# Hybrid decoder step: the first weight half between the first two row sets, two squares later

## The chip, the cores and the metric

The kernel runs on one core of a Trainium2 chip. The metric is the device time of one launch in microseconds (us). PE is TensorE, DVE is VectorE, ACT is ScalarE, POOL is GpSimd, SP is SyncE, whose queue issues most of the transfers here.

## What is computed

One layer of a decoder for a prompt of 512 rows and a sample group of 8 rows, each of width 1024. The part that matters here is the beginning: each row is normalised and multiplied with the input projection.

```python
def rms_norm(x, w):
    xf = x.astype(jnp.float32)
    y = xf * lax.rsqrt(jnp.mean(xf * xf, axis=-1, keepdims=True) + RMS_EPS)
    return (y * w.astype(jnp.float32)).astype(x.dtype)
...
    h = rms_norm(x, norm_w)
    z = jnp.einsum('bsd,de->bse', h, w_in)
    u, g_ssm, q, g_nsa, kv, gl = jnp.split(z, IN_SPLITS, axis=-1)
```

After that come a state-space scan over `u`, three branches of attention (compressed, selected and window) for prompt and sample, and one output projection with the residual.

## The kernel before, in words

The prompt's 512 rows are four row sets `xts[0..3]` of 128 rows by 1024 columns; in the listings below they are `x_66` to `x_69`. PE transposes a row set in eight 128x128 pieces (`x_transposes`), so that the 1024 columns lie on the partitions as eight slices k = 0 to 7. Two row sets together fill four PSUM banks, two with the tag `c` and two with the tag `t`; bank `t_143` can only be used once ACT has copied the transposed norm weights `nwT` out of the bank of the same tag.

Every product is computed in three matmuls of rounded parts (`mm3`, lines 121 to 123: high by high, high by low, low by high). So each operand is split in two: ACT writes the rounded high part, DVE subtracts it and writes the low part. For rows this is `x_split` (ACT `hTh`, DVE `hTl`), which multiplies with `nwT` on the way; for weights it is `w_split` (ACT `whi`, DVE `wlo`). The factor 1/rms of each row is not applied to the rows but to the results: `square` sums the squares of a row set (on ACT or DVE), `rstd_of` turns the sum into the factor with a scale on DVE and a power on POOL, and `row_table` transposes the factors so that they can be multiplied in. The sample rows `xs_in` are scaled first (`sample_scale`), transposed and split too (`sample_split`).

The first weights, 1024 by 256 columns, come in two halves (`prep_load`): k = 0 to 3 and k = 4 to 7. `u_mm` with `chan_mm(first=True)` uses them in two passes: the first over the first two row sets (`x_66`, `x_67`; 48 matmuls), the second over the other two and the sample columns (264 columns).

What sets the order: the program is written in one order, and a scheduler that is given that order and its own costs places the instructions on each engine. At the start `in_turn` binds it: each step may only be issued after the one before it on the engines of both. `issue_after` does the same for single instructions. `warm` puts matmuls without use on PE: nine at the beginning, three after the transposes of the first row set and two after those of the second. [...]

```python
square(S, ssd[0], xts[0], 128)
square(V, ssd[1], xts[1], 128)
tail = [square(S, sss, xs_in, 8)]
```

These three lines (279 to 281) put the squares of the first two row sets and of the sample rows ahead of everything in `in_turn`.

Of the kernel before, what the change touches and what calls it, by code (L numbers as in the profile page):

```python
# [26 lines left out]
C_ID, C_GRP, C_CAUS, C_CMASK, C_ROPE = 0, 128, 192, 320, 448  # L27
# [9 lines left out]
def hymba_step_kernel(  # L37
# [8 lines left out]
    nc = tc.nc  # L46
# [19 lines left out]
    V, S = PsumFirst(nc.vector), PsumFirst(nc.scalar)  # L66
# [7 lines left out]
    last = {}  # L74

    def nm(p):
        cnt[0] += 1
        return f"{p}{cnt[0]}"

    def ht(name, cols=1024, dt=F32, parts=128):  # L80
        return big.tile([parts, cols], dt, tag="H", name=nm(name), bufs=NH)

    def pt_(name, cols=1024, dt=F32, parts=128):
        return big.tile([parts, cols], dt, tag="P", name=nm(name), bufs=NP)

    def ld(name, cols=1024, dt=F32, parts=128):
        return big.tile([parts, cols], dt, tag="ld", name=nm(name), bufs=NLD)

    def wh(name, cols=1024):
        return big.tile([128, cols], F32R, tag="wh", name=nm(name), bufs=NWH)  # L90

    def st(shape, name, dt=F32, bufs=1, tag=None):
        n = nm(name)
        return sm.tile(shape, dt, tag=tag or n, name=n, bufs=bufs)
# [7 lines left out]
    def k1(name, cols=128, parts=128, dt=F32):  # L102
        return sm.tile([parts, cols], dt, tag="k1", name=nm(name), bufs=NS)
# [6 lines left out]
    def pb(use):  # L110
        tag = ROUTE[use]
        return psum.tile([128, 512], F32, tag=tag, name=nm(tag), bufs=BANKS[tag])
# [32 lines left out]
    xts = [ht("x") for _ in range(4)]  # L145
    cst = st([128, NC_CST], "cst")
    nwr = k1("nwr", 128, 8)
    xs_in = pt_("xs", parts=8)
# [6 lines left out]
    load_x = lambda i: nc.sync.dma_start(xts[i], x_prompt[0, 128 * i:128 * i + 128, :])  # L155
    nc.scalar.dma_start(nwr, norm_w.rearrange("o (a n) -> (o a) n", a=8))
    load_x(0)
    nc.sync.dma_start(cst[:, 0:128], cst_d[:, 0:128])
    load_x(1)
    nc.sync.dma_start(xs_in, x_sample[:, 0, :])  # L160
    ident = cst[:, C_ID:C_ID + 128]

    mhalf = st([128, 16], "mhalf")
    V.memset(mhalf, -0.5)
# [1 line left out]
    def rstd_of(out, ssq, n, parts, cols):  # L166
        V.tensor_scalar(out, ssq, 1.0 / n, EPS, op0=ALU.mult, op1=ALU.add)
        return G.tensor_tensor(out, out, mhalf[:parts, :cols], op=ALU.pow)  # L168
# [28 lines left out]
    p = pb("tr")  # L197
# [6 lines left out]
    def square(eng, ss, xtile, parts):  # L204
        if eng is V:
            return V.scalar_tensor_tensor(xsq[1][:parts], xtile, 1.0, xtile, op0=ALU.mult, op1=ALU.mult, accum_out=ss)
        return S.activation(xsq[0][:parts], xtile, AF.Square, accum_out=ss)
# [9 lines left out]
    def x_split(j, banks, k):  # L217
        sl = slice(256 * j, 256 * j + 256)
        p = banks[k % 4][:, 256 * (k // 4):256 * (k // 4) + 256]
        h = S.mul(hh(k)[:, sl], p, nwT[:, k:k + 1])  # L220
        return h, V.scalar_tensor_tensor(hl(k)[:, sl], p, nwT[:, k:k + 1], hh(k)[:, sl].bitcast(F32), op0=ALU.mult, op1=ALU.subtract)

    rsd = st([128, 4], "rsd")
    rsT = st([128, 512], "rsT", tag="rsT")

    w_in2 = w_in[0]

    def prep(c0, n=256, cols=None, use=None):

        return list(prep_steps(c0, n, cols, use))[-1]  # L230

    def prep_load(c0, n=256, cols=None):
        v = lambda t: t.rearrange("p (k n) -> p k n", n=n)
        parts = []
        for k0, nk in (((0, 4), (4, 4)) if n == 256 else ((0, 3), (3, 3), (6, 2))):
            raw = ld("w", nk * n)
            src = w_in2[128 * k0:128 * (k0 + nk)].rearrange("(k p) n -> p k n", p=128)
            for o, c, m in cols or ((0, c0, n),):
                last["load"] = nc.sync.dma_start(v(raw)[:, :, o:o + m], src[:, :, c:c + m])
            parts.append((raw, k0, nk))  # L240
        return parts

    def prep_steps(c0, n=256, cols=None, use=None):
        v = lambda t: t.rearrange("p (k n) -> p k n", n=n)
        tiles = []
        parts = prep_load(c0, n, cols)
        yield
        for raw, k0, nk in parts:
            if use:
                use(v(raw), k0, nk)  # L250
            hi, lo = wh("whi", nk * n), wh("wlo", nk * n)
            split(hi, lo, raw)
            tiles += [(v(hi)[:, k], v(lo)[:, k]) for k in range(nk)]
        yield tiles


    w0 = [(raw, wh("whi"), wh("wlo")) for raw, _, _ in prep_load(0)]
    load_x(2)
    load_x(3)

    def w_split(k, n):
        raw, hi, lo = w0[k // 4]
        sl = slice(256 * (k % 4), 256 * (k % 4) + 256 * n)
        h = S.copy(hi[:, sl], raw[:, sl])
        return h, V.tensor_tensor(lo[:, sl], raw[:, sl], hi[:, sl].bitcast(F32), op=ALU.subtract)
# [4 lines left out]
    ssd, sss = [st([128, 1], "ss", bufs=4, tag="ss") for _ in range(4)], st([8, 1], "ss8")  # L270
    rs = st([8, 1], "rs")
    b0 = x_banks()
# [4 lines left out]
    with tc.issue_after(last["xt"].ins):  # L277
        warm(NFILL - 1)
    square(S, ssd[0], xts[0], 128)
    square(V, ssd[1], xts[1], 128)  # L280
    tail = [square(S, sss, xs_in, 8)]
    for i in range(2):
        rstd_of(rsd[:, i:i + 1], ssd[i], 1024, 128, 1)
    rstd_of(rs, sss, 1024, 8, 1)

    def in_turn(*steps):

        for f in steps:
            with ExitStack() as s_:
                for i_ in tail:  # L290
                    s_.enter_context(tc.issue_after(i_.ins))
                new = f()
            tail[:] = list(new) if len(new) > 1 else tail if not new else [i_ for i_ in tail if i_.ins.engine != new[0].ins.engine] + list(new)
# [4 lines left out]
    def row_table(i):  # L298
        if i == 0:
            pr[0] = pb("ph")  # L300
        rb = k1("rb")
        c_ = V.tensor_copy(rb, rsd[:, i:i + 1].to_broadcast([128, 128]))
        T.transpose(pr[0][:, 128 * i:128 * i + 128], rb, ident)
        if i % 2:
            S.copy(rsT[:, 128 * i - 128:128 * i + 128], pr[0][:, 128 * i - 128:128 * i + 128])
        return (c_,)
# [12 lines left out]
    def sample_split():  # L319
        for kp in range(4):  # L320
# [5 lines left out]

    x = lambda j, b, k: lambda: x_split(j, b, k)
    w = lambda k, n: lambda: w_split(k, n)
    in_turn(x(0, b0, 0), x(0, b0, 1), w(0, 1), x(0, b0, 2), w(1, 1), x(0, b0, 3), w(2, 2), sample_scale, x(0, b0, 4), x(0, b0, 5),
            w(4, 2), lambda: row_table(0), lambda: row_table(1), x(0, b0, 6), x(0, b0, 7), w(6, 2), sample_split,  # L330
            lambda: (square(S, ssd[2], xts[2], 128),), lambda: (square(S, ssd[3], xts[3], 128),))
    b1 = x_banks()
    for i in range(2):
# [167 lines left out]
    p = pb("ac")  # L501
# [123 lines left out]
    for src, ct_ in ((c_re, CTr), (c_im, CTi)):  # L625
        cn = k2("cn", 256).rearrange("p (q n) -> p q n", n=64)
        nc.sync.dma_start(cn, src[0].rearrange("(q g) c n -> (g c) q n", q=4))
        p = pb("ac")
# [18 lines left out]
    for a, src in enumerate((state_re, state_im)):  # L647
        n0 = k1("n0")
        nc.sync.dma_start(n0, src[0].rearrange("b (a c) n -> (b a) (c n)", c=2))
        p = pb("ac")  # L650
# [312 lines left out]
    p = pb("tr")  # L963
# [794 lines left out]
```

## Time and profile before

| | |
|---|---|
| median of 3 runs | 468.19 us (467.05 to 469.04) |
| the profiled execution | 468.64 us, span 466.9 us |
| PE busy | 452.1 us, 97% of the span |
| DVE busy | 348.8 us, 75% |
| ACT busy | 241.3 us, 52% |
| POOL busy | 95.4 us, 20% |
| mean granted TensorE clock | 0.985 of full |

The span runs from the first to the last instruction of the profiled execution; its own time has a little around it. An engine's busy share is a mean over stages with different limits. Times in the rows below are counted from the start of the span.

### The profile page before, as it was taken

What the parts mean: (1) busy time and instruction counts of PE and PEld (TensorE: products, weight loads), DVE (VectorE), ACT (ScalarE), POOL (GpSimd) and SP (SyncE); (2) the same over time, 40 slices, a digit from 0 to 9 for tenths busy, and PEclk for the clock granted to TensorE, in tenths of its full rate; (3) what the DMA queues carried; (4) which work ended last, traced back from release to release, by engine and by line L of the source; (5) the groups of instructions that cost most, each with busy time, mean ns of one, the idle gap of its engine ahead of it and who ended that gap; (6) DMA issues with size and microseconds to landing.
All of it is one profiled execution on the core that took longest, in us unless ns stands there. A gap on an engine that the chain in (4) does not pass through costs nothing.

```text
span 466.9 us, 10954 instructions
## 1 busy us (share of the span) xinstructions
PE 452.1 (97%) x4258; PEld 385.9 (83%) x4258; DVE 348.8 (75%) x942; ACT 241.3 (52%) x587; POOL 95.4 (20%) x104
## 2 busy tenths in 40 slices
PE   8999999999999998799999999999899999999996
PEld 4989999899999998698686776867568799799885
DVE  6978999998998998385676858687756687683332
ACT  5913764756324328475676668566856555342100
POOL 3100000056442000462342214321433010000000
PEclk9999999999999997789999999999999999999999
DMA  8776533614627433466143362429343784311211
GB/s 290 247 225 167 84 73 108 187 40 82 143 57 214 129 82 73 148 209 187 46 140 114 121 215 79 148 90 350 104 141 130 220 209 152 101 58 58 69 46 48
DMA packets 75635, 62.84 MB, mean 135 GB/s; under 512 B 29262, under 2 KB 69056, under 8 KB 75456
## 3 DMA queue, kind: packets, MB, share of 16 engines
q1 hardware_dynamic: 66208, 36.74, 28.2%
q0 software_dynamic: 4816, 17.03, 11.5%
q10 hardware_dynamic: 4560, 8.39, 5.7%
q8 instruction: 33, 0.54, 0.5%
q14 instruction: 18, 0.15, 0.1%
HBM read 55.63 MB, written 10.70 MB: 142 GB/s over the span
## 4 chain that ended last, share of the span: by engine, by line
PE 73%; DVE 13%; DMA 7%; POOL 3%; issue 2%; ACT 1%; SPq 0%; DVEq 0%; POOLq 0%; ACTq 0%
PE a L121 11%; PE a L122 11%; PE a L123 10%; PE ph L1372 8%; DMA kvg<-in_cache_kv_dram,idx 4%; PE a L1262 4%; PE t L1253 4%; PE a L1220 3%; PE t L1348 3%; PE c L1545 3%; POOL rsq L168 2%; DVE ga L62 2%; PE t L1338 2%; PE ph L473 1%; DMA x<-in_x_prompt_dram 1%
## 5 line engine op out<-in xcount | busy, mean ns | idle before, releaser
L121 PE MATMUL a<-hTh,whi 128*128 128x256 f32 (+1 forms) x192 | 54.8, 287 | 0.6 <-DVE sg L61 0.6
L122 PE MATMUL a<-hTh,wlo 128*128 128x256 f32 (+1 forms) x192 | 54.8, 287 | 0.0
L123 PE MATMUL a<-hTl,whi 128*128 128x256 f32 (+1 forms) x192 | 53.4, 284 | 0.0
L1329 POOL DMA_INDIRECT kvg<-in_cache_kv_dram,idx x32 | 32.8, 1026 | 82.2 <-PE c L1123 40.1
L168 POOL TENSOR_TENSOR rsq<-rsq,mhalf 128x6 f32<-128x6 f32 (+3 forms) x10 | 28.7, 2872 | 101.8 <-DVE rsq L62 101.8
L122 PE MATMUL a<-whi,hTl 128*128 128x256 f32 (+1 forms) x160 | 45.8, 287 | 0.0
L123 PE MATMUL a<-wlo,hTh 128*128 128x256 f32 (+1 forms) x160 | 45.3, 284 | 0.0
L121 PE MATMUL a<-whi,hTh 128*128 128x256 f32 (+1 forms) x160 | 45.2, 287 | 0.0
L1372 PE MATMUL ph<-XT,W1h 128*128 128x256 f32 x256 | 44.5, 298 | 0.0
L61 ACT ACTIVATE P<-a,mx 128x128 f32<-128x128 f32 (+3 forms) x64 | 33.6, 533 | 13.3 <-DVE mx L61 11.5
L61 DVE TENSOR_REDUCE mx<-a 128x1 f32<-128x384 f32 (+3 forms) x48 | 27.9, 596 | 13.8 <-PE a L1221 13.6
L121 PEld LDWEIGHTS a<-hTh,whi 128*128 128x128 f32 x192 | 36.2, 188 | 1.1 <-DVE sg L61 0.8
L122 PEld LDWEIGHTS a<-hTh,wlo 128*128 128x128 f32 x192 | 36.2, 188 | 0.9 <-issue 0.4
L122 PE MATMUL a<-woh,mixl 128*128 128x256 f32 x128 | 36.1, 283 | 0.0
L121 PE MATMUL a<-woh,mixh 128*128 128x256 f32 x128 | 36.1, 284 | 0.0
L123 PE MATMUL a<-wol,mixh 128*128 128x256 f32 x128 | 36.0, 283 | 0.0
L123 PEld LDWEIGHTS a<-hTl,whi 128*128 128x128 f32 x192 | 35.7, 189 | 0.1
L1372 PEld LDWEIGHTS ph<-XT,W1h 128*128 128x128 f32 x256 | 34.9, 192 | 0.3 <-ACT XT L61 0.2
L62 ACT CAST whi<-w 128x1024 fp32r<-128x1024 f32 (+4 forms) x26 | 23.9, 927 | 15.8 <-PE a L122 10.5
L61 ACT COPY pT<-t 128x512 f32<-128x512 f32 x40 | 23.1, 588 | 15.8 <-PE t L1253 12.6
L122 PEld LDWEIGHTS a<-whi,hTl 128*128 128x128 f32 x160 | 30.1, 188 | 1.2 <-issue 0.9
L121 PEld LDWEIGHTS a<-whi,hTh 128*128 128x128 f32 x160 | 29.9, 189 | 0.9 <-PE ph L473 0.4
(410 smaller groups left out, 1235.5 us busy)
## 6 DMA issues: line engine op xcount, KB each, us to landing
w<-in_w_in_dram SPq DMA_DIRECT2D x16, 512.0 KB
out_dram<-in_cache_win_dram ACTq DMA_DIRECT2D x8, 511.0 KB
x<-in_x_prompt_dram SPq DMA_DIRECT2D x4, 512.0 KB
TT<-scr_k SPq DMA_DIRECT2D x4, 512.0 KB
w<-in_w_in_dram SPq DMA_DIRECT2D x16, 128.0 KB
W1r<-in_cmp_w_dram SPq DMA_DIRECT2D x4, 512.0 KB
wk<-in_cache_win_dram SPq DMA_DIRECT2D x8, 256.0 KB
wv<-in_cache_win_dram SPq DMA_DIRECT2D x8, 256.0 KB
```

The costliest lines, as they stand in the source:

```text
L61: return f(*args, **kw)
L62: return f(*args, **kw)
L121: T.matmul(out, ah, bh, start=start, stop=False, skip_group_check=True)
L122: T.matmul(out, al, bh, start=False, stop=False, skip_group_check=True)
L123: T.matmul(out, ah, bl, start=False, stop=stop, skip_group_check=True)
L168: return G.tensor_tensor(out, out, mhalf[:parts, :cols], op=ALU.pow)
L1220: T.matmul(bank, QTv(g, r)[:, qsl], KTv(g, a)[:, brs, :n], start=(a == 0), stop=False, skip_group_check=True)
L1253: T.transpose(p[:, 128 * r:128 * r + 128], P[r][:, br, 128 * kt:128 * kt + 128], ident)
L1262: mm = T.matmul(po[64 * br:64 * br + 64, :], kvt[kt - 1][:, c0:c0 + 64], behind[kt - 1][br][0], start=(kt == 1), stop=(kt == i + 1), tile_ ...
L1329: G.indirect_dma_start(out=gt_, out_offset=None, in_=ckv, in_offset=bass.IndirectOffsetOnAxis(ap=idx[:, 2 * pr_ + b2, jq:jq + 1], axis=0))
L1348: T.transpose(p[:, 256 * g + 128 * b2:256 * g + 128 * b2 + 128], gts[jq][b2][:, o:o + 128], ident)
L1372: T.matmul(ph3[:, kd], (W1l if part == 1 else W1h)[kd][a][:, wsl], (xl if part == 2 else xh)[:, e, a:a + 256], start=(jq == 0 and kd == 0 ...
```

## The change

The transfer of the first half of the weights is issued ahead of the second row set, and the second half behind it; `prep_load` gets a hook between its two halves for that. The sample rows are fetched after both. In `in_turn` the splits of k = 0 to 3 of the weights now stand ahead of all splits of rows, and the squares of the second row set (DVE) and of the sample rows (ACT), with the two factors that come out of them, have become a step of `in_turn` behind the split of k = 4 and 5 of the weights. The rest of the diff is code that only stands at another line.

```diff
-    load_x(1)
-    nc.sync.dma_start(xs_in, x_sample[:, 0, :])
...
-    def prep_load(c0, n=256, cols=None):
+    def prep_load(c0, n=256, cols=None, between=None):
...
             parts.append((raw, k0, nk))
+            if between:
+                between()
+                between = None
         return parts
+    first_w = prep_load(0, between=lambda: load_x(1))
+    nc.sync.dma_start(xs_in, x_sample[:, 0, :])
...
-    w0 = [(raw, wh("whi"), wh("wlo")) for raw, _, _ in prep_load(0)]
+    w0 = [(raw, wh("whi"), wh("wlo")) for raw, _, _ in first_w]
...
     square(S, ssd[0], xts[0], 128)
-    square(V, ssd[1], xts[1], 128)
-    tail = [square(S, sss, xs_in, 8)]
-    for i in range(2):
-        rstd_of(rsd[:, i:i + 1], ssd[i], 1024, 128, 1)
-    rstd_of(rs, sss, 1024, 8, 1)
+    tail = []
+    rstd_of(rsd[:, 0:1], ssd[0], 1024, 128, 1)
+    def rows_squared():
+        i_ = square(V, ssd[1], xts[1], 128), square(S, sss, xs_in, 8)
+        rstd_of(rsd[:, 1:2], ssd[1], 1024, 128, 1)
+        rstd_of(rs, sss, 1024, 8, 1)
+        return i_
...
-    in_turn(x(0, b0, 0), x(0, b0, 1), w(0, 1), x(0, b0, 2), w(1, 1), x(0, b0, 3), w(2, 2), sample_scale, x(0, b0, 4), x(0, b0, 5),
-            w(4, 2), lambda: row_table(0), lambda: row_table(1), x(0, b0, 6), x(0, b0, 7), w(6, 2), sample_split,
+    in_turn(w(0, 1), w(1, 1), w(2, 2), x(0, b0, 0), x(0, b0, 1), x(0, b0, 2), x(0, b0, 3), x(0, b0, 4), w(4, 2), rows_squared,
+            x(0, b0, 5), sample_scale, lambda: row_table(0), lambda: row_table(1), x(0, b0, 6), x(0, b0, 7), w(6, 2), sample_split,
```

How the order moves on ACT, from its first square on (`w_124` and `w_82` are the first half of the weights, `w_126` and `w_85` the second, `c_140` to `t_143` the banks of transposed rows). Before:

```order
L62 ACTIVATE xsq_120,ss_134<-x_66 128x1024
L62 ACTIVATE xsq_120,ss_138<-xs_72 8x1024
L61 COPY nwT_118<-t_116 128x8
L61 ACTIVATE hTh_108<-c_140,nwT_118 128x256
L61 ACTIVATE hTh_108<-t_141,nwT_118 128x256
L62 CAST whi_128<-w_124 128x256
L61 ACTIVATE hTh_109<-c_142,nwT_118 128x256
```

With the change:

```order
L62 ACTIVATE xsq_124,ss_134<-x_66 128x1024
L62 CAST whi_128<-w_82 128x256 x2
L62 CAST whi_128<-w_82 128x512
L61 COPY nwT_122<-t_120 128x8
L61 ACTIVATE hTh_112<-c_140,nwT_122 128x256
L61 ACTIVATE hTh_112<-t_141,nwT_122 128x256
L61 ACTIVATE hTh_113<-c_142,nwT_122 128x256
L61 ACTIVATE hTh_113<-t_143,nwT_122 128x256
L61 ACTIVATE hTh_114<-c_140,nwT_122 128x256
L62 CAST whi_130<-w_85 128x512
L62 ACTIVATE xsq_124,ss_138<-xs_72 8x1024
```

The three casts of the first half have moved ahead of the copy `nwT`, and the square of the sample rows has moved behind five row splits and a cast.

On PE, from the last transpose of `x_66` that needs no `nwT` (`wz` are the fill matmuls). Before:

```order
L213 MATMUL c_142<-cst_70,x_66 128x128
L213 MATMUL c_140<-cst_70,x_67 128x128
...
L213 MATMUL c_142<-cst_70,x_67 128x128
L213 MATMUL t_143<-cst_70,x_66 128x128 x2
L177 LDWEIGHTS wz_86
L177 MATMUL ph_88<-wz_86 128x512
...
L213 MATMUL t_143<-cst_70,x_67 128x128 x2
```

With the change:

```order
L230 MATMUL c_142<-cst_70,x_66 128x128
L230 MATMUL t_143<-cst_70,x_66 128x128 x2
L194 LDWEIGHTS wz_90
L194 MATMUL ph_92<-wz_90 128x512
...
L230 MATMUL c_140<-cst_70,x_67 128x128
L230 MATMUL t_141<-cst_70,x_67 128x128
L230 MATMUL c_142<-cst_70,x_67 128x128
L230 MATMUL t_143<-cst_70,x_67 128x128
```

Six transposes of `x_67` have moved from ahead of `t_143` and the three fill matmuls to behind them.

On SP, the first transfers (`cst_70` is the table of constants, `xs_72` the sample rows). Before:

```order
L155 DMA x_66<-in_x_prompt_dram 128x1024
L158 DMA cst_70<-in_constants_dram 128x128
L155 DMA x_67<-in_x_prompt_dram 128x1024
L160 DMA xs_72<-in_x_sample_dram 8x1024
L239 DMA w_124<-in_w_in_dram 128x4x256
L239 DMA w_126<-in_w_in_dram 128x4x256
```

With the change:

```order
L155 DMA x_66<-in_x_prompt_dram 128x1024
L158 DMA cst_70<-in_constants_dram 128x128
L170 DMA w_82<-in_w_in_dram 128x4x256
L155 DMA x_67<-in_x_prompt_dram 128x1024
L170 DMA w_85<-in_w_in_dram 128x4x256
L178 DMA xs_72<-in_x_sample_dram 8x1024
```

One half of the weights has moved ahead of `x_67`, the other ahead of the sample rows.

## Rows read from the trace of the kernel before

**Rows 1.** The page, part 4: the chain that ended last, shares by engine.

```profile
PE 73%; DVE 13%; DMA 7%; POOL 3%; issue 2%; ACT 1%; SPq 0%; DVEq 0%; POOLq 0%; ACTq 0%
```

**Rows 2.** The chain in order of time: start us, us, what.

```profile
1.64 5.81 DMA x<-in_x_prompt_dram
...
10.95 0.12 PE a L122
...
13.74 0.59 PE ph L314 x8
...
14.91 0.44 PE t L213 x4
...
98.83 1.15 DVE pt L62 x2
```

**Rows 3.** Timeline of PE, 6 to 19 us: start us, us, what, [idle before].

```profile
6.49 0.42 PE L213 MATMUL c<-cst,x 128*128 128x128 f32 x1
7.49 0.33 PE L213 MATMUL c<-cst,x 128*128 128x128 f32 x1 [0.58 <-DMA x<-in_x_prompt_dram]
...
8.58 0.44 PE L213 MATMUL t<-cst,x 128*128 128x128 f32 x2 [0.21 <-ACT nwT L61]
8.86 0.81 PE L177 MATMUL ph<-wz 128*128 128x512 bf16 x3
9.50 0.38 PE L213 MATMUL t<-cst,x 128*128 128x128 f32 x2
...
9.96 0.47 PE L121 MATMUL a<-hTh,whi 128*128 128x256 f32 x1
...
19.00 0.29 PE L121 MATMUL a<-hTh,whi 128*128 128x264 f32 x1
```

**Rows 4.** Timeline of ACT, 7 to 14 us.

```profile
7.33 1.06 ACT L62 ACTIVATE xsq<-xs 8x1024 f32<-8x1024 f32 x1 [1.71 <-DMA xs<-in_x_sample_dram]
...
8.39 0.14 ACT L61 COPY nwT<-t 128x8 f32<-128x8 f32 x1
8.56 0.47 ACT L61 ACTIVATE hTh<-c,nwT 128x256 fp32r<-128x256 f32 x1
...
9.29 0.40 ACT L62 CAST whi<-w 128x256 fp32r<-128x256 f32 x1
9.58 0.49 ACT L61 ACTIVATE hTh<-c,nwT 128x256 fp32r<-128x256 f32 x1
...
10.61 0.64 ACT L62 CAST whi<-w 128x512 fp32r<-128x512 f32 x1
11.12 0.50 ACT L61 ACTIVATE hTh<-c,nwT 128x256 fp32r<-128x256 f32 x1
...
13.59 1.11 ACT L62 ACTIVATE xsq<-x 128x1024 f32<-128x1024 f32 x1
```

**Rows 5.** Timeline of DVE, 7 to 16 us.

```profile
7.47 1.23 DVE L62 SCALAR_TENSOR_TENSOR xsq<-x 128x1024 f32<-128x1024 f32 x1 [1.67 <-DMA x<-in_x_prompt_dram]
...
9.07 0.48 DVE L61 SCALAR_TENSOR_TENSOR hTl<-c,nwT,hTh 128x256 fp32r<-128x256 f32 x1 [0.17 <-ACT hTh L61]
...
11.31 0.68 DVE L62 TENSOR_TENSOR wlo<-w,whi 128x512 fp32r<-128x512 f32 x1
...
15.05 0.67 DVE L62 TENSOR_TENSOR wlo<-w,whi 128x512 fp32r<-128x512 f32 x1
```

**Rows 6.** Busy time by stretch: stretch, length, engines, granted clock, DMA share, GB/s.

```profile
7.45:9.29 1.84, 1.59 (x11) 1.11 (x12) 1.65 (x5) 1.81 (x6) 0.45 (x1) 1.00 1.09 392
```

**Rows 7.** Timeline of PE after two idle times, and the granted clock near them.

```profile
178.58 0.54 PE L995 MATMUL a<-identr,qs 128*128 128x128 f32 x4 [1.22 <-DVE qs L62]
...
180.90:187.60 6.70, 6.70 (x59) 6.22 (x59) 4.96 (x25) 5.78 (x21) 0.00 (x0) 0.50 0.22 47
194.60:201.30 6.70, 5.06 (x30) 4.88 (x31) 3.30 (x8) 3.37 (x12) 4.46 (x6) 0.50 0.78 256
...
195.73 0.48 PE L1338 MATMUL t<-cst,kvg 128*128 128x128 f32 x1 [2.77 <-DMA kvg<-in_cache_kv_dram,idx]
```

More of the change, by code (lines that the diff above doesn't have):

```diff
@@ L158, in hymba_step_kernel @@
     nc.sync.dma_start(cst[:, 0:128], cst_d[:, 0:128])
-    load_x(1)
+    ident = cst[:, C_ID:C_ID + 128]
+    w_in2 = w_in[0]
+    def prep_load(c0, n=256, cols=None, between=None):
+        v = lambda t: t.rearrange("p (k n) -> p k n", n=n)
+        parts = []
+        for k0, nk in (((0, 4), (4, 4)) if n == 256 else ((0, 3), (3, 3), (6, 2))):
+            raw = ld("w", nk * n)
+            src = w_in2[128 * k0:128 * (k0 + nk)].rearrange("(k p) n -> p k n", p=128)
+            for o, c, m in cols or ((0, c0, n),):
+                last["load"] = nc.sync.dma_start(v(raw)[:, :, o:o + m], src[:, :, c:c + m])
+            parts.append((raw, k0, nk))
+            if between:
+                between()
+                between = None
+        return parts
+    first_w = prep_load(0, between=lambda: load_x(1))
     nc.sync.dma_start(xs_in, x_sample[:, 0, :])
-    ident = cst[:, C_ID:C_ID + 128]
     mhalf = st([128, 16], "mhalf")
@@ L224, in hymba_step_kernel @@
     rsT = st([128, 512], "rsT", tag="rsT")
-    w_in2 = w_in[0]
     def prep(c0, n=256, cols=None, use=None):
         return list(prep_steps(c0, n, cols, use))[-1]
-    def prep_load(c0, n=256, cols=None):
[L233 to L241, printed above, removed]
     def prep_steps(c0, n=256, cols=None, use=None):
```

## The prediction

> **What bounds the kernel now.** I read the page first. TensorE (PE) holds 73% of the chain that ended last [rows 1], so the question is always when PE gets its work and whether it then stands still. The chain of waits over the whole span comes next [rows 2]. Its first long piece is the transfer of the second row set, `x_67`, which lands at 7.45; the first long piece off PE after that starts at 98.83. A shift of PE in the first 20 us is therefore carried on, and I take it to be carried to the end.
>
> The timeline of the start shows what PE does with that landing [rows 3]. Six transposes of `x_66` end about 6.9, and the ones of `x_67` start at 7.49, behind a wait for the transfer. At 8.58 the last two transposes of `x_66` start, behind a wait for ACT's small copy `nwT`. The first real matmul follows at 9.96 and the second pass at 19.00. ACT is busy without a gap from 8.56 to 13.59: eight scaled copies of rows (`hTh`), two 256-wide and three 512-wide casts of weights [rows 4]. DVE runs the matching list from 9.07 to the split at 15.05 [rows 5].
>
> **The change, part by part.**
>
> *The transfers.* The first half of the first weights, `w_82`, now stands in the queue where `x_67` stood, with the same 512 KB, so I let it land at 7.45 [rows 2]. `x_67` comes one such transfer later: 524 KB at the 392 GB/s of that stretch [rows 6] is 1.34 us, so 8.8. The other half, `w_85`, and the sample rows are one more behind, about 10.2; ACT wants them at 11.8 and 12.3 (below). `x_68` and `x_69` have the same bytes ahead of them as before. Nothing is added to the queues.
>
> *ACT.* Between the square of `x_66` and `nwT` there now stand three casts of `w_82` instead of the square of the sample rows. From one start to the next a 256-wide cast takes 0.29 (9.29 to 9.58) and a 512-wide one 0.51 (10.61 to 11.12) [rows 4]. 7.45 + 0.29 + 0.29 + 0.51 = 8.54, and `nwT` with its 0.14 ends at 8.68. Before it ended at 8.53: this wait has only changed its cause.
>
> *PE until the first matmul.* In the new order the two `t_143` transposes of `x_66` and three fill matmuls stand ahead of all eight transposes of `x_67`. The two start at 8.72, the fills 0.28 later (8.58 to 8.86), the transposes of `x_67` another 0.64 later (8.86 to 9.50) [rows 3], so at 9.64, although their rows landed at 8.8. Two transposes and two fills took 0.46 until the first matmul (9.50 to 9.96); six more transposes at 0.11 (four take 0.44 [rows 2]) add 0.66. First matmul: 10.76, which is 0.8 later than before.
>
> *PE from there to the second pass.* It has 48 matmuls at 0.12, sixteen transposes at 0.11, eight of the sample rows in 0.59 [rows 2] and two of the row tables, taken at 0.11: 5.76 + 1.76 + 0.59 + 0.22 = 8.33. Before, this took 9.04 (9.96 to 19.00 [rows 3]), the rest being waits for splits. Now the splits of the first four weight slices are done before any row arrives, and PE should run through: 10.76 + 8.33 = 19.1. I allow 0.3 for small waits: 19.4, or **0.4 later** than before.
>
> *What covers this.* ACT starts `hTh` at about 9.95. Its list is the old one of 5.03 us (thirteen instructions) [rows 4] less 1.09 for the three casts, plus 1.06 for the sample square, so it ends at 15.0; one `hTh` is 0.37, the last comes at 14.5, and PE reaches that slice after 17. DVE starts 0.5 behind ACT, at 10.45. Its list of 6.6 us (9.07 to 15.65, taking the last split until its 512-wide pitch of 0.60 is over) loses the splits of `w_82` (about 1.3, of which the 512-wide row shows 0.68) and gains the square of `x_67`, 1.23 [rows 5]; it ends about 17.1. PE comes to that last split after six slices of 0.72, sixteen transposes and the sample's: 10.76 + 4.32 + 0.12 + 1.76 + 0.59 = 17.55. The cover is 0.4 us. If DVE is later than that (it waits for POOL's power of the sample rows on the way), each tenth is paid by PE.
>
> *The second pass.* The sample columns' split now stands on ACT behind four row splits of the second half instead of two. ACT: 15.0, two squares at about 1.25, four `hTh` at 0.37 give 19.0; four small copies, at most 0.14 each as for `nwT` [rows 4], then the same on DVE and one row split. PE asks for that result at 19.9 and gets it between 19.8 and 20.4. I take 0.2 if PE is on time, nothing if it is later.
>
> *The clock.* PE is now idle from 6.9 to 8.72, 1.8 us in one piece; before it was 0.6 and a little more at 8.4. The trace has two such places later [rows 7]. [...] An idle time of 1.8 lies between the two. The price lies between 0 (no fall) and half of 6.7, that is 3.35 us, if PE had dense work throughout. I take **1.2**: nearer to the low end than the middle, because in the first of those stretches PE ran many tiny matmuls and in the second it idled on, whereas here 256-wide matmuls follow at once, as in the fill at the start, after which the clock was up. [...]
>
> *The sum.* With the fall PE is late enough not to wait in the second pass: 0.4 + 1.2 = **1.6 us slower**. The profiled execution took 468.64 for its span of 466.9, so 470.2; it lies 0.45 above the median of the runs, 468.19, and on that median the forecast is **469.8 us**. A measurement here can tell about 0.5%, or 2.3 us, from no change; the forecast stays inside that.
>
> **The rivals.**
>
> *No fall of the clock.* For it: one fill of idle time differs from the next, the idle 0.6 at 6.9 did no harm [rows 3], and the two falls came in stretches that were thin around the idle time as well. Against it: the lengths above. Then 0.4 + 0.2 = 0.6: 468.8.
>
> *The clock stays down as long as in the two later stretches* (the slower side). Its place is PE from about 10 to 16.7, its price 3.35 + 0.4 = 3.75: 471.9, over the bound. It decides from the point where the low stretch lasts longer than about 3.9 us, since 0.4 + 1.95 is 2.35. For it speak the two rows, both 6.7 long; against it, that both held idle or tiny work.
>
> *The order in the queue does not order the landings.* All transfers share the 16 engines, so `w_82` may land only together with `x_67`, at 8.8. Then the early splits have no gap to fill, `nwT` comes 1.3 later and PE with it; what PE does not make up in the first pass, about 1.2 beside the 0.4, stays: 469.8 without a fall of the clock. That the x transfer ahead, in the same place, landed at 7.45 speaks against it.
>
> *The later order.* The scheduler moved instructions on PE, DVE and ACT far behind the start, also where the chain runs over DVE (13%) and POOL (3%, about 14 us) [rows 1]. I cannot price the swaps one by one; a fifth of POOL's part, 3 us, either way: 465.2 to 471.2. For it: the chain leaves PE there [rows 2]. Against it: PE has no lack of work at those places.
>
> **How the numbers follow.** Chances: forecast 0.46, no fall 0.24, long fall 0.15, joint landing 0.07, later order 0.08. Slower by over 0.5% takes nearly all of the long fall (0.14), the upper part of the forecast, whose clock price may be 0.8 higher (0.10), and some of the last two (0.04): 0.28. Faster by over 0.5% is left to the later order (0.05) and to chance beside the no-fall case (0.02): 0.07. The rest, 0.65, is no change. The range reaches from the no-fall case less 1.5 (later order, an earlier landing of `w_82`) to the long fall and 0.4 beyond: 467.3 to 472.3. It leaves out most of the later order's faster side, 0.05, the top of the long fall, 0.06, and some 0.05 of the others.
>
> **What would show it.** Right: ACT casts `whi` before `nwT`, starting near 7.45; `nwT` ends about 8.7; `x_67` is awaited no later than 8.8; the first matmul stands near 10.8 and the second pass near 19.4, or near 20.6 with 128-wide transposes or 256-wide matmuls at twice their spacing for a few us after 9. Wrong: casts that start much before or after 7.45; a first matmul before 10; PE waiting for a weight split inside the first pass; or a second pass that starts as computed while the end differs by more than 2 us from it, which would put the cause behind 98.

## The result and the profile after

The changed kernel took **470.40 us** (median of 17 runs, 468.02 to 475.51), the kernel before, run beside it, 468.75 (17 runs, 465.51 to 472.93): ratio 1.0051, 95% interval 1.0028 to 1.0075. By the ratio that is 2.4 us slower (1.3 to 3.5), which leaves out no change; the medians differ by 1.65. The ratio is not that of the medians, and it leaves out runs more than 1.5% above the fastest of their kernel. The profiled execution took 469.86 for a span of 468.1; before it was 468.64 for 466.9.

The timeline of PE in the changed kernel, at the start and then every wait over 0.3 us from 25 to 186 us:

```profile
6.01 0.27 PE L230 MATMUL c<-cst,x 128*128 128x128 f32 x1
9.04 0.69 PE L230 MATMUL t<-cst,x 128*128 128x128 f32 x2 [2.75 <-ACT nwT L61]
9.52 1.49 PE L194 MATMUL ph<-wz 128*128 128x512 bf16 x3
10.80 0.42 PE L230 MATMUL c<-cst,x 128*128 128x128 f32 x1
11.01 0.42 PE L230 MATMUL t<-cst,x 128*128 128x128 f32 x1
...
12.71 0.44 PE L121 MATMUL a<-hTh,whi 128*128 128x256 f32 x1
...
21.41 0.37 PE L121 MATMUL a<-hTh,whi 128*128 128x264 f32 x1
...
55.47 0.62 PE L638 MATMUL c<-cst,cn 128*64 128x128 f32 x4 [0.63 <-DMA cn<-in_ssm_c_re_dram]
...
64.86 0.39 PE L121 MATMUL a<-whi,hTh 128*128 128x256 f32 x1 [0.52 <-ACT kvt L61]
...
138.80 0.39 PE L121 MATMUL a<-hTh,whi 128*128 128x264 f32 x1 [1.16 <-DVE sg L61]
...
178.64 1.35 PE L790 MATMUL t<-HB,WY 64*64 64x72 f32 x64 [0.82 <-DVE HB L62]
...
182.59 0.54 PE L1003 MATMUL a<-identr,qs 128*128 128x128 f32 x4 [0.51 <-DVE qs L62]
...
184.06 0.62 PE L1010 MATMUL a<-identr,ks 128*128 128x128 f32 x3 [0.50 <-DVE ks L62]
```

The first matmul moved from 9.96 to 12.71 and the second pass from 19.00 to 21.41 [rows 3]. Ahead of `t_143` PE idles 2.75 us for `nwT`; the fills and the transposes of `x_67` behind it then run at half pace (from 9.52 to 10.80 for three fills, before 8.86 to 9.50). ACT does what the order says, the casts first:

```profile
7.69 1.23 ACT L62 CAST whi<-w 128x256 fp32r<-128x256 f32 x3 [2.36 <-DMA w<-in_w_in_dram]
8.83 0.16 ACT L61 COPY nwT<-t 128x8 f32<-128x8 f32 x1
12.18 0.47 ACT L61 ACTIVATE hTh<-c,nwT 128x256 fp32r<-128x256 f32 x1 [3.19 <-PE c L230]
```

Busy time by stretch (the number ahead of the last two is the granted clock): it is down to 0.50 of full between about 9 and 12.3 us. In the two later stretches in which it had fallen before [rows 7] it stayed up in this execution, almost or wholly:

```profile
8.00:10.00 2.00, 0.96 (x4) 0.63 (x5) 1.46 (x3) 0.99 (x4) 0.00 (x0) 0.73 1.07 405
10.00:12.00 2.00, 2.00 (x9) 1.53 (x8) 0.00 (x0) 0.00 (x0) 0.00 (x0) 0.50 1.02 391
12.00:14.00 2.00, 2.00 (x14) 1.64 (x13) 1.31 (x4) 1.82 (x6) 0.00 (x0) 0.92 1.10 355
180.90:187.60 6.70, 5.49 (x75) 4.69 (x74) 6.41 (x23) 5.81 (x20) 0.00 (x0) 1.00 0.32 63
194.60:201.30 6.70, 3.81 (x31) 3.17 (x30) 1.70 (x5) 3.78 (x14) 4.53 (x6) 0.91 0.88 280
```

The chain that ended last, by engine on the page, where PE held 73% before [rows 1]:

```profile
PE 63%; DVE 14%; DMA 13%; issue 3%; POOL 2%; SPq 2%; ACT 2%; DVEq 0%; POOLq 0%; ACTq 0%
```

Behind the start the kernel before waits only at two such places up to 186 us: 1.22 for `qs` [rows 7], and this one, from its timeline of PE:

```profile
135.14 0.39 PE L121 MATMUL a<-hTh,whi 128*128 128x264 f32 x1 [0.58 <-DVE sg L61]
```

So two marks serve for all runs below: the start of the **second pass**, and the start of the transposes of **`qs`** (178.58 before, 182.59 now). The first came 2.4 later. The second came 4.0 later, so another 1.6 was lost in between: the listing above shows at which waits, and the table how much they come to. From there to the end of the span the profiled execution won back 2.8; in a second one (e10, below) it won back 0.4.

| run | second pass | `qs` | between | PE's waits, 25 to 186 us | ratio to before, 95% |
|---|---|---|---|---|---|
| before | 19.00 | 178.58 | 159.58 | 1.80 | |
| changed | 21.41 | 182.59 | 161.18 | 4.14 | 1.0051, 1.0028 to 1.0075 |
| e1 `nwT` first | 20.88 | 182.76 | 161.88 | 5.13 | 1.0053, 1.0029 to 1.0077 |
| e2 gap filled | 21.77 | 182.03 | 160.26 | 3.68 | 1.0102, 1.0068 to 1.0137 |
| e3 turn only | 19.68 | 180.01 | 160.33 | 3.68 | 1.0045, 1.0015 to 1.0074 |
| e4 transfers only | 23.79 | 183.20 | 159.41 | 1.72 | 1.0084, 1.0051 to 1.0117 |
| e5 squares only | 19.20 | 181.35 | 162.15 | 5.24 | 1.0023, 0.9996 to 1.0049 |
| e6 `w` first | 20.30 | 179.56 | 159.26 | 1.68 | 1.0007, 0.9977 to 1.0037 |
| e7 `nwT` in before | 18.71 | 178.06 | 159.35 | 1.76 | 1.0007, 0.9978 to 1.0037 |
| e8 gap filled, pinned | 20.21 | 181.09 | 160.88 | 4.15 | 1.0068, 1.0040 to 1.0097 |
| e9 start delayed | 28.57 | 187.91 | 159.34 | 1.75 | 1.0191, 1.0151 to 1.0231 |
| e10 changed again | 22.14 | 183.26 | 161.12 | 4.32 | 1.0107, 1.0058 to 1.0155 |
| e11 as e8 | 19.77 | 180.70 | 160.93 | 4.06 | 1.0072, 1.0045 to 1.0100 |
| e12 as e5 | 18.50 | 179.25 | 160.75 | 3.60 | 1.0024, 0.9992 to 1.0056 |

Times of a row are from its one profiled execution in us; "between" is the difference of the two before it; the waits are PE's idle times of 0.15 us or more, added (for e9 up to its `qs`). One execution differs from another of the same kernel by more than these steps: the changed kernel's lay between 468.0, at a mean granted clock of 0.996, and 475.5, at 0.973. Two profiles of one kernel (changed and e10, e5 and e12, e8 and e11) differ by 0.4 to 0.7 at the second pass. So the marks tell where time goes, and the ratios how much of it arrives. In the nine rows that have the changed kernel's later order of matmuls (all but before, e4, e6, e7 and e9) `qs` stands 2.9 later than before on average, and the ratios come to 2.8 us on average, though in a single row the two differ by up to 1.7.

### The profile page after: what moved, and what is told of

The parts are those of the page before. It is cut to its first block, busy times and chain, and to the rows that moved or that the text cites. A ratio compares the mean times of both kernels' runs of the same rounds, so it can differ in the third digit from the quotient of the medians.

```text
span 468.1 us, 10953 instructions
## 1 busy us (share of the span) xinstructions
PE 449.8 (96%) x4258; PEld 383.3 (82%) x4258; DVE 349.4 (75%) x942; ACT 241.8 (52%) x587; POOL 94.3 (20%) x104
## 4 chain that ended last, share of the span: by engine, by line
PE 63%; DVE 14%; DMA 13%; issue 3%; POOL 2%; SPq 2%; ACT 2%; DVEq 0%; POOLq 0%; ACTq 0%
PE a L121 9%; PE a L122 9%; PE a L123 9%; PE ph L1380 8%; DMA kvg<-in_cache_kv_dram,idx 4%; PE a L1270 4%; PE t L1261 3%; PE a L1228 3%; PE t L1356 2%; DMA yT<-scr_y 2%; DMA w<-in_w_in_dram 2%; PE c L1553 2%; PE t L1346 2%; SPq L419 2%; DVE wlo L62 2%
## 5 line engine op out<-in xcount | busy, mean ns | idle before, releaser
L185 POOL TENSOR_TENSOR rsq<-rsq,mhalf 128x6 f32<-128x6 f32 (+3 forms) x10 | 27.4, 2746 | 103.0 <-DVE rsq L62 103.0
L62 DVE TENSOR_TENSOR wlo<-w,whi 128x1024 fp32r<-128x1024 f32 (+4 forms) x26 | 27.4, 1062 | 4.6 <-ACT whi L62 4.5
```

What stands on the lines that cost most here:

```text
L62: return f(*args, **kw)
```

## The experiments

The listings of e1, e2, e3 and e8 show the edit against the changed kernel, those of e5, e6, e7 and e9 against the kernel before.

### Only the place of `nwT` (e1)

```diff
-    S.copy(nwT, p[:, 0:8])
+    nw_copy = S.copy(nwT, p[:, 0:8])
...
-    tail = []
+    tail = [nw_copy]
```

> The changed kernel, but the copy of nwT is issued on ACT ahead of the three casts of w_82. Theory (the copy behind the casts leaves PE idle for 2.75 us, the clock falls, and both together make the loss): nwT ends near 5.6, t_143 is transposed near 6.2, the three fills end near 7.1, PE waits for x_67 until about 8.8, the first matmul stands near 10.2 (changed kernel 12.71) and the second pass near 19.1 (21.41), so about 2.3 us less than the changed kernel: ratio to before near 1.000. Rival one (only the later landing of x_67 counts): the second pass stays later than 20.5 and the ratio near 1.005. Rival two (the loss lies in the order behind 98 us): the second pass comes earlier, but the ratio stays near 1.005. Open within the theory is whether the 1.7 us that remain idle ahead of x_67 let the clock fall too; then the transposes of x_67 stand 0.21 apart and the second pass near 20.3.

The wait did not go, it changed its name. The first cast on ACT, then the timeline of PE:

```profile
8.20 1.23 ACT L62 CAST whi<-w 128x256 fp32r<-128x256 f32 x3 [2.79 <-DMA w<-in_w_in_dram]
...
9.53 0.33 PE L230 MATMUL c<-cst,x 128*128 128x128 f32 x1 [2.98 <-DMA x<-in_x_prompt_dram]
...
10.93 0.58 PE L121 MATMUL a<-hTh,whi 128*128 128x256 f32 x1
...
20.88 0.37 PE L121 MATMUL a<-hTh,whi 128*128 128x264 f32 x1
```

`x_67` landed only at 9.5, not at 8.8, and behind an idle time of 2.98 the clock fell all the same, now under the first pass (0.71 in 10 to 12, 0.50 in 12 to 14). The second pass came 0.5 earlier, not 2.3, which is no more than two profiles of one kernel differ, and the ratio stayed. The theory's first half fell: taking `nwT` from behind the casts wins next to nothing, because with it out of the way the row set itself is late.

### Only the idle time of PE (e2, e8, e11)

```diff
-        for k in range(8):
+        for k in (0, 1, 2, 4, 5, 6, 3, 7) if (j, i) == (0, 0) else range(8):
...
+            if (j, i, k) == (0, 0, 3):
+                with tc.issue_after(last["xt"].ins):
+                    warm(12)
```

> The changed kernel with twelve more fill matmuls on PE between the sixth transpose of x_66 and the two that wait for nwT; ACT, DVE and the transfers are as in the changed kernel. Theory (part of the loss is the clock, which falls because PE idles): PE is busy from 6.3 to about 8.85, the granted clock stays at 1.00 through 8 to 14, the transposes of x_67 stand 0.11 apart, nwT still ends near 9.0, the first matmul comes near 11.1 instead of 12.71 and the second pass near 19.9 instead of 21.41: ratio to before near 1.002. Rival (the wait for nwT and x_67 alone makes the loss, the clock costs nothing at the end): the second pass stays past 21 and the ratio near 1.005.

The clock stayed at 1.00, and the first matmul came 1.0 earlier (11.69), but the second pass came at 21.77 and the ratio was 1.0102. The added fills had shifted the scheduler's order on DVE: its first operation on the constants stood earlier and waited, with the row splits behind it. The timeline of DVE:

```profile
16.60 0.17 DVE L62 TENSOR_SCALAR kk<-cst 128x16 f32<-128x16 f32 x1 [1.07 <-DMA cst<-in_constants_dram]
```

So the run was repeated with that operation bound behind the last split of the first weights, which `last["ws"]` holds (e8, and once more as e11):

```diff
-    V.tensor_scalar(kk8[:, 0:16], cst[:, C_BLK:C_BLK + 16], 8.0, None, op0=ALU.mult)
+    with tc.issue_after(last["ws"].ins):
+        V.tensor_scalar(kk8[:, 0:16], cst[:, C_BLK:C_BLK + 16], 8.0, None, op0=ALU.mult)
```

> As the run with the gap filled (twelve more fill matmuls ahead of the transposes that wait for nwT), but DVE's first operation on the constants (kk) is bound behind the last split of the first weights, where it stands in the changed kernel, so that DVE does not wait for the constants in the first pass. Theory (the clock is a part of the start's loss): granted clock 1.00 from 6 to 20, first matmul near 11.7 as in that run, second pass near 20.4 (21.77 there, 21.41 in the changed kernel), idle times between 25 and 186 near 3.7, ratio to before 1.002 to 1.004. Rival (the clock's fall has no price, since PE waits for the splits in any case): second pass past 21.2, ratio 1.005.

> The kernel with the gap filled and kk bound, once more: 1.0068 was above the changed kernel though its second pass came 1.2 us earlier. If the clock's fall at the start costs what it takes from the second pass, the ratio should lie 0.0025 below the changed kernel's, near 1.003. If the ratio is again at or above the changed kernel's, the 1.2 us gained at the start do not reach the end, and the profile should show a lower granted clock or more idle time between 180 and 210 us that takes them back.

PE in e8:

```profile
9.26 0.44 PE L233 MATMUL t<-cst,x 128*128 128x128 f32 x2 [0.94 <-ACT nwT L61]
...
10.18 0.27 PE L233 MATMUL c<-cst,x 128*128 128x128 f32 x1
10.29 0.27 PE L233 MATMUL t<-cst,x 128*128 128x128 f32 x1
...
11.52 0.39 PE L121 MATMUL a<-hTh,whi 128*128 128x256 f32 x1
...
20.21 0.37 PE L121 MATMUL a<-hTh,whi 128*128 128x264 f32 x1
```

From the two transposes to the first matmul it is 2.26 at a granted clock of 1.00; in the changed kernel, with 0.50 behind the idle time, the same work took 3.67 (9.04 to 12.71). So the fall of the clock costs 1.4 at the start, and the second pass duly came 1.2 (e8) and 1.6 (e11) earlier. But the ratios, 1.0068 and 1.0072, expected near 1.003, lie between the changed kernel's two, 1.0051 and 1.0107. The intervals overlap too widely to say that the gain is lost, and nothing shows that it arrives. In e8 the granted clock fell between 180 and 200 (0.75 and 0.84; in e11 0.60 and 0.84), where the changed kernel's profile had 1.00; in e10 it fell there in the changed kernel too. That remains open.

### Only the order of the steps (e3)

```diff
-    first_w = prep_load(0, between=lambda: load_x(1))
+    load_x(1)
     nc.sync.dma_start(xs_in, x_sample[:, 0, :])
+    first_w = prep_load(0)
```

> The new order of the splits and the later squares, with the transfers in the order of before (x_67, xs, then the weights). Theory (the start decides, and the new order by itself neither gains nor loses much): nwT is copied near 5.5, x_67 is transposed from 7.5, the casts of the first half start near 9.2 when it has landed and hold the row splits back to 10.4, the first matmul stands near 10.9 and the second pass near 19.5; ratio to before 1.000 to 1.002. Rival one (the order of the splits and squares is what costs 2.4 us, on DVE and ACT): the second pass past 21, ratio near 1.005. Rival two (the new order is a gain that the transfers spoil): second pass at 18.5 or earlier, ratio 0.999 or less.

The second pass came at 19.68, near the theory's 19.5, and yet the ratio is 1.0045, nearly as large as the whole change's. Between the marks lie 160.33, in line with the other runs with the new order (160.26 to 162.15). This was the first sign of a second loss.

### Only the transfers (e4, e6)

e4 has the diff's fetch order with the old `in_turn` and the squares in their old place.

> The transfers of the change (w_82, x_67, w_85, then xs) with the splits and squares in the order of before. Theory (the start decides by what ACT has to wait for): nwT is copied near 5.5, but the square of the sample rows, which stands ahead of all splits, now waits for xs until about 10.4 and ends near 11.5; PE has transposed x_67 by 9.8 and idles to about 12.1, so its clock falls, and the second pass comes near 21.5; ratio to before near 1.005. Rival (the transfers are harmless and the order of the splits makes the loss): first matmul near 10.8, second pass near 19.4, ratio 1.001 or less.

As expected, though later, ACT's square of the sample rows waited for its transfer (it starts at 11.09) and PE for ACT, as its timeline shows:

```profile
13.29 0.38 PE L121 MATMUL a<-hTh,whi 128*128 128x256 f32 x1 [2.51 <-ACT whi L62]
...
23.79 0.29 PE L121 MATMUL a<-hTh,whi 128*128 128x264 f32 x1
```

The second pass came 4.8 later (2.5 were expected), the waits behind it are those of before (1.72), and the ratio is 1.0084, about 3.9 us. In e6 the sample rows are fetched ahead of both halves, so that nothing waits for them:

```diff
-    load_x(1)
     nc.sync.dma_start(xs_in, x_sample[:, 0, :])
+    first_w = prep_load(0, between=lambda: load_x(1))
```

> The kernel before, with the first half of the weights fetched ahead of x_67 and the second half behind it; the sample rows are fetched ahead of both, so that their square holds nothing back; splits and squares as before. New theory: only the start is lost. x_67 lands near 9.3 instead of 7.4, PE idles about 2 us ahead of it, the first matmul stands near 11 and the second pass near 20.7 (1.7 later than before, of which about 1 if the clock stays up); PE's idle times between 25 and 186 us stay at 1.8; ratio to before 1.002 to 1.004. Rival (the fetch order is harmless, the casts and squares make the loss): second pass at 19.4 or earlier, ratio 1.000.

PE's timeline in e6:

```profile
6.90 0.44 PE L229 MATMUL t<-cst,x 128*128 128x128 f32 x2 [0.86 <-ACT nwT L61]
...
8.98 0.33 PE L229 MATMUL c<-cst,x 128*128 128x128 f32 x1 [1.00 <-DMA x<-in_x_prompt_dram]
...
11.03 0.38 PE L121 MATMUL a<-hTh,whi 128*128 128x256 f32 x1 [0.52 <-ACT whi L62]
...
20.30 0.29 PE L121 MATMUL a<-hTh,whi 128*128 128x264 f32 x1
...
136.16 0.39 PE L121 MATMUL a<-hTh,whi 128*128 128x264 f32 x1 [0.47 <-DVE sg L61]
...
179.56 0.54 PE L999 MATMUL a<-identr,qs 128*128 128x128 f32 x4 [1.21 <-DVE qs L62]
```

`nwT` is early here, `t_143` and the fills split the idle time into 0.86 and 1.00, and the clock stayed at 1.00. What is left is the later `x_67`: second pass 1.3 later, and behind it the waits of before. The ratio, 1.0007, is below the 1.002 that was expected; its interval holds no change and 1.3 us alike.

### Only the squares (e5, e12)

```diff
-    S.copy(nwT, p[:, 0:8])
+    nw_copy = S.copy(nwT, p[:, 0:8])
...
-    square(V, ssd[1], xts[1], 128)
-    tail = [square(S, sss, xs_in, 8)]
+    tail = [nw_copy]
...
+    in_turn(x(0, b0, 0), x(0, b0, 1), w(0, 1), x(0, b0, 2), w(1, 1), x(0, b0, 3), w(2, 2), x(0, b0, 4), w(4, 2), rows_squared,
+            x(0, b0, 5), sample_scale, lambda: row_table(0), lambda: row_table(1), x(0, b0, 6), x(0, b0, 7), w(6, 2), sample_split,
```

With the two squares go the factors that come out of them and the scaling of the sample rows, and `nwT` is bound ahead of the splits as in e1.

> Transfers and the order of the splits as in the kernel before; only the squares of x_67 and of the sample rows, with the scaling of the sample rows, stand later, at the change's place. New theory (two losses: the start, and a later order that the scheduler chooses once the squares stand late): the start is as good as before, first matmul at 9.7 to 10.0 and second pass at 19.3 or earlier, yet PE's idle times between 25 and 186 us add up to about 3.7 us, as in the changed kernel and the runs with its order, and not to 1.8 as before; ratio to before 1.003 to 1.005. Rival (all of the loss comes from the start): idle times of 1.8, ratio 0.999 to 1.001.

> The kernel with only the squares later, once more, to narrow its interval (1.0023, 0.9996 to 1.0049). If the later order costs what its profile shows between the second pass and the transposes of qs (162.15 us against 159.58 before), ratio 1.004 or more; if that is made up behind 180 us, ratio 1.001 or less. Its profile again shows idle times of PE between 25 and 186 us above 3.5.

PE in e5:

```profile
19.20 0.36 PE L121 MATMUL a<-hTh,whi 128*128 128x264 f32 x1
...
54.18 0.63 PE L638 MATMUL c<-cst,cn 128*64 128x128 f32 x4 [1.60 <-DMA cn<-in_ssm_c_re_dram]
...
63.55 0.39 PE L121 MATMUL a<-whi,hTh 128*128 128x256 f32 x1 [0.65 <-ACT kvt L61]
...
137.53 0.39 PE L121 MATMUL a<-hTh,whi 128*128 128x264 f32 x1 [1.18 <-DVE sg L61]
...
177.40 1.35 PE L790 MATMUL t<-HB,WY 64*64 64x72 f32 x64 [0.78 <-DVE HB L62]
```

With transfers and splits as before, the start is that of before (19.20 and 18.50), and yet the same waits stand at the same places as in the changed kernel. In all fourteen traces PE runs the same 1714 matmuls between the two marks. In e5 and e12 they stand in the changed kernel's order, one for one, while in e4, e6, e7 and e9 they stand in the order of before. The early `nwT` (e7) and the fetch order with its moved code (e4, e6) thus leave the order alone. So the late squares, with what goes with them, make the scheduler choose another order for the next 160 us. Up to `qs` it costs 0.9 to 2.8 us in nine profiles (160.26 to 162.15) against 159.26 to 159.58 in the five with the old order; most of that spread is the wait for `cn`, between nothing and 1.60 from run to run. Without that wait the nine lie between 160.26 and 160.57, so the part of the price that every run shows is about 1 us. The two ratios, 1.0023 and 1.0024, make about 1.1 us, between the two cases expected for e12, and each interval just reaches no change: the price is shown at the marks, not at the end.

### The other way round: `nwT` early in the kernel before (e7)

```diff
-    tail = [square(S, sss, xs_in, 8)]
+    with tc.issue_after(nw_copy.ins):
+        tail = [square(S, sss, xs_in, 8)]
```

> The kernel before, with the copy of nwT issued ahead of the square of the sample rows on ACT, nothing else. Theory: PE no longer waits 0.21 us for nwT and has t_143 earlier, but its matmuls still wait for the row splits behind the square of the sample rows: second pass 0 to 0.3 earlier than 19.0, the later idle times 1.8, ratio 0.999 to 1.000. Rival (the wait for nwT holds much more than its 0.21 us): second pass at 18.3 or earlier, ratio 0.998 or less.

Second pass 18.71, 0.3 earlier, ratio 1.0007: as the theory said, nothing that can be measured. No run here beats the kernel before.

### How much of a late start arrives (e9)

```diff
-NWARM, NFILL = 9, 3
+NWARM, NFILL = 41, 3
```

> The kernel before with 32 more fill matmuls ahead of everything on PE (41 instead of 9), 0.21 us each: PE begins its transposes 6.8 us later, stays busy meanwhile, and the order behind the start is that of before. It measures how much of a late start reaches the end. If all of it does: second pass near 24.5, the transposes of qs (before 178.58) as much later as the second pass, and the end 5 to 6 us later, ratio 1.011 to 1.013. If half of it is made up later (other waits end at their own time): ratio near 1.006. If the stretch from 180 to 210 us absorbs it: ratio 1.003 or less, with less idle time of PE at the gathers there.

The delay came out larger than planned: the splits begin only when PE has transposed, so PE then waited for DVE, and the clock fell behind that (0.66 in 20 to 25). PE's timeline:

```profile
18.59 0.39 PE L122 MATMUL a<-hTh,wlo 128*128 128x256 f32 x1 [2.62 <-DVE wlo L62]
...
28.57 0.29 PE L121 MATMUL a<-hTh,whi 128*128 128x264 f32 x1
...
187.91 0.53 PE L995 MATMUL a<-identr,qs 128*128 128x128 f32 x4 [1.21 <-DVE qs L62]
```

The second pass came 9.6 later, `qs` 9.3, and the end 8.9 (1.0191 of 468.43; the interval makes it 7.1 to 10.8). So most of a late start arrives. How nearly all is not shown: the marks are those of one execution, the fastest of the six, whose span of 472.4 is only 5.5 longer than that of before.

### The changed kernel again (e10)

> The changed kernel once more, beside the others on one chip, to hold its ratio against theirs: near 1.005 as before; in its profile idle times of PE between 25 and 186 us near 4 again and the second pass near 21.4. If the idle time ahead of the cn products near 55 differs much from 0.63, that wait varies from execution to execution and is no fixed part of the later order's price.

The waits are there again (4.32, with 0.66 for `cn`), PE's idle time for `nwT` was 3.22 and the clock down from 8 to 14, so the second pass came at 22.14. `qs` stood 4.7 later than before and the span, 471.2, was 4.3 longer. The clock by stretch shows what the first profiled execution had been spared:

```profile
180.00:190.00 10.00, 8.99 (x133) 7.91 (x123) 8.31 (x35) 7.71 (x24) 0.00 (x0) 0.76 0.37 77
190.00:200.00 10.00, 9.86 (x164) 9.22 (x163) 4.75 (x16) 4.18 (x13) 2.04 (x2) 0.73 0.10 22
```

The two intervals of the change, 1.0028 to 1.0075 and 1.0058 to 1.0155, overlap from 2.7 to 3.5 us.

## Why the prediction was right, and where not

The forecast was 1.6 us slower, at 469.8 us, and the time of 470.40 lies inside its range; of the ways named, the one with a falling clock happened. That the medians differ by 1.65, almost the forecast, is luck. In the profiles `qs` stands 4.0 and 4.7 later, because one term of the sum was too small and another was put at nothing, and what follows `qs` gave part of it back in the first.

- *The transfers.* `w_82` came at 7.7 instead of 7.45. `x_67` was taken at 8.8; where PE waited for it, its first transpose started at 9.53 (e1), 9.26 (e4) and 8.98 (e6). The price of one transfer, 1.34, held where both landings can be seen: 8.20 to 9.53 in e1. So the two did not land together, though the transfers share the 16 engines: before, from 7.45 to 9.29, those of queue q1 alone took 108.3% of the engines' span by the profile. What varies is the landing ahead of it: the first work on `x_67` or `w_82`, whichever stood there, began between 6.62 (`x_67` in e7) and 8.20. In the changed kernel PE came to `x_67` only at 10.80, so this term cost it nothing.
- *ACT.* The order was right. `nwT` ended at 8.99 instead of 8.68, and the transposes behind it started at 9.04 instead of 8.72.
- *The idle time* was 2.75, not 1.8: 0.3 by the later `nwT`, the rest because the transposes of `x_66` stood 0.11 apart and ended at 6.3, while before most of them stood 0.21 apart and the sixth ended at 6.9 [rows 3]; the granted clock is 1.00 there in both traces, so what set them apart is not shown.
- *The clock.* It fell, as forecast: to 0.50 of full, behind an idle time of 2.75. The price was a little too small: taken 1.2, an estimate from the two stretches of 6.7 us at 0.50 [rows 7], measured 1.4 in the changed kernel's first profile by the comparison with e8, and more in e10, where the low level lasted beyond 14 us (0.50 from 12 to 14, 0.96 from 14 to 20). The argument for it was weaker than it looked: of five profiles with the order of before, all with an idle time of 1.21 or 1.22 at `qs`, the clock fell behind it in three (in 180 to 190 it is 0.66 before, 0.76 in e4, 0.59 in e7) and stayed up in e6 and e9 (1.00).
- *From the first matmul to the second pass* 8.70 (12.71 to 21.41), forecast 8.33 and 0.3 of small waits: right. DVE's cover of 0.4 (its terms add up to an end at 17.0, not 17.1) shrank but held: the last split was done at 19.77, and PE took it at 19.89.
- *The sum at the second pass* was 19.4 without and 20.6 with the clock; measured 21.41. Of the 2.0 above 19.4, 0.3 is `nwT`, 1.6 the slower stretch from 9.04 to 12.71: 1.4 for the clock, and 0.2 because the same work took 2.26 at the full clock (e8), not 2.04.
- *Carried to the end*: e9 puts it at 7.1 to 10.8 of 9.6, so most of it.
- *The later order* is the step that failed. The prediction saw that the order behind the start had changed and set it to zero, with a chance of 0.08 either way, because "PE has no lack of work at those places". It had looked at the places off PE in the chain; the 1.22 ahead of `qs` [rows 7] was a sign that PE does wait. PE now waits 4.1 us instead of 1.8, for `cn`, `kvt`, `sg`, `HB`, `qs` and `ks`. Up to `qs` this costs 1.6, two fifths of the 4.0 lost by then, and the first cause of it is the late squares (e5, e12), not the fetch.

That the ratio came out at 2.4 us and not at 4 the first time is not settled. Behind `qs` the clock falls in eleven of the fourteen profiles (0.59 to 0.76 in 180 to 190); the three without the fall there (1.00) are the changed kernel's first, e6 and e9. From `qs` to the end these three take 283.7 to 285.5 us and the eleven 286.6 to 290.0, so that stretch can give or take more than the missing 1.6. How often the fall comes in the runs without a profile is not shown.

## What to carry to other kernels

Where a scheduler places the instructions, moving two of them can rearrange everything behind: compare the built order to the far end, and count the waits of the engine that bounds in every stretch, before a step is called local. What a transfer put ahead of another one costs is to be looked for at what needed the other: `x_67` came 1.33 behind `w_82` (e1), and the first half of the weights came in time for splits that nobody waited for, while PE stood waiting. And where one kernel's runs differ by 1.6%, marks inside the trace, taken in several profiles, tell causes apart that ratios cannot.

## What the runs showed of the hardware

PE's granted clock was 0.50 behind idle times of 2.75 (the changed kernel, 10 to 12), 3.22 (e10, 8 to 14) and 2.98 us (e1, 12 to 14) at the start. It was 1.00 behind 0.86 and 1.00 with transposes and fills between them (e6, 8 to 20), where fills took all of the gap but 0.94 (e8, 8 to 20), and behind 1.49 (e12, 8 to 20). With 2.40 and 2.51 around a few transposes (e4) it was still 1.00 from 8 to 14 and 0.72 in the six microseconds behind, when dense matmuls had begun: there the fall came late and hit the work behind the idle time. At 0.50 the 128x128 transposes of `x_67` stood 0.21 apart (the changed kernel, from 10.80), at 1.00 0.11 (e8, from 10.18).

The length of the idle time alone did not decide here. In e7, e6 and e9 PE runs the same matmuls in the same order from the second pass to 5 us behind `qs`, and idles 1.22, 1.21 and 1.21 us ahead of it. Busy time and granted clock from 2.3 to 9.0 us behind the start of `qs`, in this order:

```profile
180.36:187.06 6.70, 6.70 (x57) 6.07 (x56) 4.32 (x21) 4.86 (x18) 0.00 (x0) 0.50 0.22 47
181.86:188.56 6.70, 6.56 (x134) 6.18 (x134) 6.55 (x29) 6.43 (x23) 0.00 (x0) 1.00 0.23 48
190.21:196.91 6.70, 6.40 (x129) 5.99 (x129) 6.20 (x29) 6.44 (x23) 0.00 (x0) 1.00 0.23 50
```

The clock fell in e7 and stayed up in the other two; what decides between them stays open.
